# One core of Trainium2: a conditioned decoder block put in source order, with its side work on one paced list

## The chip, the cores and the metric

The kernel runs on one core of a Trainium2 chip. A core has TensorE (matrix products), VectorE (DVE in the profile), ScalarE (ACT), GpSimd (POOL, hardly used here) and SyncE (SP), whose queue issues nearly all transfers. The metric is the device time of one execution in microseconds (us); lower is better.

## The reference, cut to what matters

```python
mod = silu(c) @ w_ada + b_ada                    # c: 4096 numbers, w_ada: 4096 x 12288
shift, scale, gate = split(mod, 3)
h = rmsnorm(x) * norm_g * (1 + scale) + shift    # x: 256 tokens x 4096 channels
a_b, a_c, a_x, a_z, b_v, b_g, b_z = split(h @ w_in)   # 4096 -> 7 x 2048
y_a = a_b * conv3(a_c * a_x) * silu(a_z)         # causal, per channel, width 3
u   = conv31(b_v * sigmoid(b_g)) + bias          # causal, per channel, width 31
y_b = silu(layernorm(u)) * silu(b_z)
x   = x + gate * ([y_a, y_b] @ w_out)            # 4096 -> 4096
return rmsnorm(x) * final_g
```

Everything is float32. Each factor of the large products is split into a high and a low part, and three of the four products of parts are summed, so that one tile of 128 input channels, 128 tokens and 512 output columns costs three TensorE products.

## The kernel before, in words

The input projection has 28 output column tiles `e` of 512 columns and 32 channel tiles `k` of 128 channels. It is not run column by column: `BLOCKS` cuts the 32 channel tiles into six blocks, and in each block all 28 column tiles take in that block's channels, so that the conditioning of a channel tile (`modT`, `gscT`) is needed only when its block begins. `_segments` lists these segments. A segment that goes on with sums of an earlier block starts from the stored sum: `seed` copies `acc[e]` into PSUM on ScalarE, and `take` copies the finished segment back out on ScalarE. Even and odd blocks walk the columns in opposite directions, and the first columns of blocks 0 and 1 stop short by `EARLY`.

A step is one load of weights for two channel tiles (`KD` = 2), 512 KB, and twelve products. `load_w` (lines 131 to 140) issues the load on SP, makes the high part on ScalarE (line 138) and the low part on VectorE (line 139). `products` (142 to 153) issues the twelve products. There are 448 steps for the input projection and 64 for each half of the output projection.

Other work lies beside it. `ada_steps` (179 to 191) computes one column of silu(c) @ w_ada for 128 outputs: four pieces of 1024 rows, each a 512 KB load and one multiply-and-sum pass on VectorE (line 189). 64 such columns are shift and scale (`mod`), 32 are `gate`. `make_h` (233 to 247) turns two channel tiles of x into h. `x_stats` (252 to 272) finds the root mean square by token from the transposed x: squares on ScalarE, sums on VectorE, a product with ones. `glu_B`, `conv_tap`, `norm_B`, `gate_B` and `silu_gate_A` work on finished columns; the width-31 convolution is 120 taps of four ScalarE passes (line 350) and one VectorE add (line 351).

The Python code hands out this work by step: `queue` holds pairs of step and function, and `run_due` calls what is due. The mod pieces are spread so that each channel tile is ready two steps before use, the gate pieces over 170 steps that begin with the last block (`GATE_RUN`), the taps from the first GLU to 43 steps behind the input projection. The tile framework then orders each engine's instructions by its own priorities; that order can differ from the source's. Mod pieces, gate pieces, weights and most x tiles share the seven buffers of `raws`; `big` has 33 slots of 4 KB per partition for h, sums and everything else.

Of the kernel before, what the change touches and what calls it, by code (L numbers as in the profile page):

```python
# [60 lines left out]
def _segments():  # L61
# [23 lines left out]
def decoder_block(ctx: ExitStack, tc: tile.TileContext, x, c, w_mod, w_gate, w_in, w_out, xt, pk, final_g, out):  # L85
    nc = tc.nc
    const = ctx.enter_context(tc.tile_pool(name="const", bufs=1))
    const.tile([P, 420], F32, name="pad")
# [4 lines left out]
    split = ctx.enter_context(tc.tile_pool(name="split", bufs=3))  # L93
# [19 lines left out]
    pks = const.tile([P, PK], F32, name="pks")  # L113
    nc.scalar.dma_start(pks, pk)
# [6 lines left out]
    def rsqrt(y, v, t):  # L121

        nc.scalar.activation(out=t, in_=v, func=AF.Sqrt)
        nc.vector.reciprocal(out=y, in_=t)
        nc.vector.tensor_tensor(out=t, in0=y, in1=y, op=ALU.mult)
        nc.vector.tensor_tensor(out=t, in0=t, in1=v, op=ALU.mult)
        nc.vector.tensor_scalar(out=t, in0=t, scalar1=-0.5, scalar2=1.5, op0=ALU.mult, op1=ALU.add)
        nc.vector.tensor_tensor(out=y, in0=y, in1=t, op=ALU.mult)


    def load_w(src, k0, name, keep=False):
        raw = rawt(f"{name}_r")
        nc.sync.dma_start(raw, src[k0 // KD])
        if keep:
            hi, lo = (bigt(f"{name}_{t}", (P, KD, CT), F32R) for t in "hl")
        else:
            hi, lo = (split.tile([P, KD, CT], F32R, tag=t, name=f"{name}_{t}") for t in "hl")
        nc.scalar.copy(hi, raw)  # L138
        nc.vector.tensor_tensor(out=lo, in0=raw, in1=hi.bitcast(F32), op=ALU.subtract)  # L139
        return hi, lo  # L140

    def products(ps, act, parts, k0, first, last, tokens=range(NS), seeded=False):

        hi, lo = parts
# [19 lines left out]
    pts = [const.tile([P, 4], F32, name=f"part{i}") for i in range(4)]  # L164
    part_no = itertools.count()
    cB = cbc.tile([P, D], F32, name="cB")
    hT = {}

    def broadcast_c():

        for q in range(D // ROW):
            row = bigt(f"crow{q}", (P, ROW))
            nc.sync.dma_start(row[:1], c[:, q * ROW:(q + 1) * ROW])
            ps = pmm.tile([P, NS, CT], F32, tag="ps", name=f"cps{q}")
            for h in range(2):
                nc.tensor.matmul(ps[:, h], ones[:1], row[:1, h * CT:(h + 1) * CT], start=True, stop=True)  # L176
            nc.scalar.activation(out=cB[:, q * ROW:(q + 1) * ROW], in_=ps, func=AF.Silu)

    def ada_steps(name, srcs, bias, dst):

        state = {}

        def step(q):
            raw = rawt(f"{name}_{q}", (P, ROW))
            nc.sync.dma_start(raw, srcs[q])
            if q == 0:
                state["part"] = pts[next(part_no) % 4]
            p = state["part"]
            nc.vector.tensor_tensor_reduce(out=raw, in0=raw, in1=cB[:, q * ROW:(q + 1) * ROW], scale=1.0, scalar=p[:, q - 1:q] if q else bias, op0=ALU.mult, op1=ALU.add, accum_out=dst if q == D // ROW - 1 else p[:, q:q + 1])  # L189

        return [lambda q=q: step(q) for q in range(D // ROW)]

    def mod_steps(k):

        def finish():
# [6 lines left out]
        return work + [finish]  # L202
# [4 lines left out]
    def gate_finish():  # L207
# [69 lines left out]
    for f in first_steps[:-4]:  # L277
        f()
# [344 lines left out]
```

## Time and profile before

| | us |
|---|---|
| median of 3 runs | 1744.9 (1743.64 to 1745.33) |
| profiled execution | 1744.85 |
| its span, first to last instruction | 1743.0 |
| TensorE busy in it | 1644.6 (94%) |
| VectorE busy | 1421.8 (82%) |
| ScalarE busy | 1163.6 (67%) |
| bytes moved | 524.51 MB, 301 GB/s in the mean |

Busy time of TensorE includes the overlap of neighbouring products, so it says less about the pace than the distance between two starts. Shares are means over stages that differ, and the rows below are cut by stage for that reason.

### The profile page before, as it was taken

The numbers are of one execution on the slowest core, as the hardware profiler recorded it, in microseconds if no ns is written. First come the engines' busy times: TensorE is split into PE (matmuls) and PEld (weight loads), VectorE is DVE, ScalarE is ACT, GpSimd is POOL, SyncE is SP. The second block draws the span as 40 slices with busy tenths as digits, with TensorE's granted clock in tenths as the row PEclk, the third lists the DMA queues.
The fourth block names the chain that finished last, engine by engine and source line by source line (L and its number), as shares of the span: only waits on it lengthen the run. The fifth ranks groups of instructions, "written<-read, shape, count | busy, mean of one in ns | idle before, by whom it ended". The sixth has DMA issues, their size and how long they took to land.

```text
span 1743.0 us, 20848 instructions
## 1 busy us (share of the span) xinstructions
PE 1644.6 (94%) x7073; PEld 1323.9 (76%) x7073; DVE 1421.8 (82%) x1707; ACT 1163.6 (67%) x1558; POOL 1.0 (0%) x8
## 2 busy tenths in 40 slices
PE   4799999999999999999999999989998999999997
PEld 1577788888888888888888777766666777778885
DVE  6887777877777777787776899999999999976675
ACT  4555966577666556566556599998898777464453
POOL 0000000000000000000000000000000000000000
PEclk9999999999999999999999999999999999999999
DMA  8998999999999999999998998868887999679663
GB/s 318 319 363 322 325 328 343 321 335 326 327 317 343 330 322 320 324 342 313 333 326 308 332 304 286 300 220 273 271 266 264 314 314 320 221 273 321 201 201 149
DMA packets 146771, 524.51 MB, mean 301 GB/s; under 512 B 16196, under 2 KB 16228, under 8 KB 146664
## 3 DMA queue, kind: packets, MB, share of 16 engines
q1 hardware_dynamic: 146520, 522.81, 86.1%
q8 instruction: 55, 0.90, 0.2%
q10 hardware_dynamic: 144, 0.37, 0.1%
q14 instruction: 52, 0.43, 0.1%
HBM read 518.91 MB, written 4.21 MB: 300 GB/s over the span
## 4 chain that ended last, share of the span: by engine, by line
PE 63%; DVE 18%; issue 10%; ACT 5%; DMA 4%; DVEq 0%; ACTq 0%
PE ps L152 17%; PE ps L153 17%; PE ps L151 17%; DVE w_l L139 5%; DVE cv L351 5%; DVE gate L189 3%; PE pb L151 3%; PE pb L153 3%; PE pb L152 3%; DMA mod<-in_w_mod 2%; ACT w_h L138 2%; ACT pr L350 1%; DVE mod L189 1%; DMA gate<-in_w_gate 1%; PE cps L176 1%
## 5 line engine op out<-in xcount | busy, mean ns | idle before, releaser
L139 DVE TENSOR_TENSOR w_l<-w_r,w_h 128x1024 fp32r<-128x1024 f32 x576 | 702.7, 1226 | 236.1 <-ACT w_h L138 234.3
L138 ACT CAST w_h<-w_r 128x1024 fp32r<-128x1024 f32 x576 | 600.2, 1048 | 260.1 <-PE ps L153 140.7
L152 PE MATMUL ps<-w_l,hT 128*128 128x512 f32 x1792 | 709.4, 396 | 26.5 <-DVE w_l L139 26.3
L151 PE MATMUL ps<-w_h,hT 128*128 128x512 f32 x1792 | 703.4, 393 | 27.6 <-ACT hT L157 18.1
L153 PE MATMUL ps<-w_h,hT 128*128 128x512 f32 x1792 | 703.6, 393 | 1.1 <-DVE hT L158 1.1
L152 PEld LDWEIGHTS ps<-w_l,hT 128*128 128x128 f32 x1792 | 339.2, 189 | 115.4 <-DVE w_l L139 46.2
L151 PEld LDWEIGHTS ps<-w_h,hT 128*128 128x128 f32 x1792 | 339.5, 190 | 104.0 <-ACT hT L157 19.2
L153 PEld LDWEIGHTS ps<-w_h,hT 128*128 128x128 f32 x1792 | 339.6, 190 | 71.9 <-DVE hT L158 3.2
L446 ACT ACTIVATE acc<-ps 128x1024 f32<-128x1024 f32 x163 | 167.4, 1027 | 223.0 <-PE ps L153 222.6
L189 DVE CUSTOM_DVE_ANT_0 mod<-mod,cB,part 128x1024 f32<-128x1024 f32 x192 | 245.7, 1280 | 26.0 <-DMA mod<-in_w_mod 24.1
L350 ACT ACTIVATE pr<-uT,pks 128x255 f32<-128x255 f32 (+14 forms) x480 | 197.0, 488 | 1.8 <-DVE cv L351 1.6
L351 DVE TENSOR_TENSOR cv<-cv,pr 128x1020 f32<-128x1020 f32 (+14 forms) x120 | 140.3, 1169 | 3.6 <-ACT pr L350 3.4
L438 ACT COPY ps<-acc 128x1024 f32<-128x1024 f32 x135 | 137.0, 1016 | 0.4
L189 DVE CUSTOM_DVE_ANT_0 gate<-gate,cB,part 128x1024 f32<-128x1024 f32 x96 | 124.2, 1294 | 1.6 <-DMA gate<-in_w_gate 1.5
L152 PE MATMUL pa<-w_l,yT 128*128 128x512 f32 x256 | 104.0, 406 | 7.9 <-DVE w_l L139 7.4
L151 PE MATMUL pa<-w_h,yT 128*128 128x512 f32 x256 | 100.3, 394 | 1.8 <-ACT w_h L138 1.8
L153 PE MATMUL pa<-w_h,yT 128*128 128x512 f32 x256 | 100.9, 394 | 0.0
L151 PE MATMUL pb<-w_h,yT 128*128 128x512 f32 x256 | 99.7, 389 | 0.0
L152 PE MATMUL pb<-w_l,yT 128*128 128x512 f32 x256 | 99.6, 389 | 0.0
L153 PE MATMUL pb<-w_h,yT 128*128 128x512 f32 x256 | 99.6, 389 | 0.0
L189 DVE CUSTOM_DVE_ANT_0 mod<-mod,cB,pks 128x1024 f32<-128x1024 f32 x64 | 81.9, 1280 | 12.3 <-DMA mod<-in_w_mod 12.3
L152 PEld LDWEIGHTS pa<-w_l,yT 128*128 128x128 f32 x256 | 48.7, 190 | 27.4 <-DVE w_l L139 17.6
(122 smaller groups left out, 678.5 us busy)
## 6 DMA issues: line engine op xcount, KB each, us to landing
w_r<-in_w_in SPq DMA_DIRECT2D x448, 512.0 KB, 5.0
mod<-in_w_mod SPq DMA_DIRECT2D x256, 512.0 KB, 5.1
gate<-in_w_gate SPq DMA_DIRECT2D x128, 512.0 KB, 4.6
w_r<-in_w_out SPq DMA_DIRECT2D x128, 512.0 KB, 4.6
xs<-in_xt SPq DMA_DIRECT2D x8, 512.0 KB, 10.0
xr<-in_x SPq DMA_DIRECT2D x8, 512.0 KB, 6.7
out<-o SPq DMA_DIRECT2D x16, 256.0 KB, 2.9
xc<-in_xt SPq DMA_DIRECT2D x10, 256.0 KB, 4.6
```

What stands on the lines that cost most here:

```text
L138: nc.scalar.copy(hi, raw)
L139: nc.vector.tensor_tensor(out=lo, in0=raw, in1=hi.bitcast(F32), op=ALU.subtract)
L151: nc.tensor.matmul(out, ah, hi[:, i], start=f, stop=False, skip_group_check=seeded)
L152: nc.tensor.matmul(out, ah, lo[:, i], start=False, stop=False, skip_group_check=seeded)
L153: nc.tensor.matmul(out, al, hi[:, i], start=False, stop=l, skip_group_check=seeded)
L176: nc.tensor.matmul(ps[:, h], ones[:1], row[:1, h * CT:(h + 1) * CT], start=True, stop=True)
L189: nc.vector.tensor_tensor_reduce(out=raw, in0=raw, in1=cB[:, q * ROW:(q + 1) * ROW], scale=1.0, scalar=p[:, q - 1:q] if q else bias, op0=A ...
L350: nc.scalar.activation(out=pr[:, j, sh:], in_=u[:, j, :S - sh], func=AF.Copy, scale=cbw[:, 4 * i + j, TAPS - 1 - sh:TAPS - sh])
L351: nc.vector.tensor_tensor(out=o[:, :, sh:], in0=o[:, :, sh:], in1=pr[:, :, sh:], op=ALU.add)
L438: nc.scalar.copy(ps, acc[e])
L446: nc.scalar.activation(out=acc[e], in_=ps, func=AF.Silu if k1 == KT and e >= 24 else AF.Copy)
```

## The change

All engines now run in the order of the source (last lines of the diff), and the source is rewritten so that each piece of side work is a step of its own at a set time. Time is counted in units `now` of one channel tile (six products); 896 units are the input projection, 128 each half of the output projection.

- Blocks are (2, 4, 4, 6, 8, 8); in the first block the first fifteen columns take in channel tile 0 alone (`ALONE`). A step has one or two tiles; a load of one tile is 256 KB.
- Weights are loaded two steps ahead instead of one (`AHEAD`). Weights have four buffers of their own (`raws`), the pieces of w_ada three of 8 KB per partition (`rows`); a piece has 2048 rows, 1 MB. x tiles for h now lie in `big`, which has 34 slots.
- All pieces after channel tile 0, mod first and gate behind it, are one list, `filler`. `run_due` takes the next piece when it is due (on the line `hull`, ahead of all needs) or when two running counts allow it: `vec`, VectorE's planned work, and `load`, the planned transfers at `RATE` MB per us, both against the planned time `FIRST + UNIT * now`.
- h is made in five separate steps of set leads (`H_LEAD`); the taps, the normalisation and the gating of A and B are cut up in the same way, with a producer on one engine and its consumer on the next put some units apart.
- Row statistics of x come from x in its natural layout: squares on ScalarE with a sum by token (`accum_out`), the reciprocal root on 128 x 2 numbers, and two products that spread it over the partitions. They stand between the passes that make `cB`.
- Silu and sigmoid of finished columns are applied while the sum leaves PSUM (`take`), not as passes of their own. Activation tables are asked for ahead of use (`table`).
- In the second half of the output projection the sums start from the first half's (`seed_b`), in place of an add afterwards. The gate vector is stored through ScalarE's queue instead of SP's.

```diff
-BLOCKS = (4, 4, 4, 6, 6, 8)
-
-EARLY = {0: 12, 1: 10}
+BLOCKS = (2, 4, 4, 6, 8, 8)
+
+ALONE = 15
+EARLY = {1: 14}
 KD = 2
-AHEAD = 1
-LEAD = 2
-KEEP = 3
+AHEAD = 2
+ROW = 2048
 HOLD = 5
-ROW = 1024
-GATE_RUN = (0, 170)
-A_SPAN = 5
-
-CONV_END = 43
-NORM_AT = 45
-NORM_SPAN = 20
-LOAD_AT = 1
-TILE_SPAN = 4
+
+
+UNIT = 1.363
+FIRST = 29.0
+RATE = 0.385
+W_LOAD = 0.2622
+ADA_LOAD = 1.0486
+LOW_PART = 0.57
+ADA_SUM = 2.42
+SLACK = 3.0
+
+
+H_LEAD = (9, 6, 4, 2, 1)
+H_DUE = 8
+A_STEP = 3
+CONV_END = 86
+NORM_AT = 88
+NORM_STEP = 2
+LOAD_AT = 2
+TILE_STEP = 3
...
+            if b == 0 and n < ALONE:
+                k1 = 1
...
+def _steps(k0, k1):
+
+    cuts = [k0] + [k for k in range(k0 + 1, k1) if k % KD == 0] + [k1]
+    return [(a, b - a) for a, b in zip(cuts, cuts[1:])]
...
-    big = ctx.enter_context(tc.tile_pool(name="big", bufs=33))
+    big = ctx.enter_context(tc.tile_pool(name="big", bufs=34))
+    raws = ctx.enter_context(tc.tile_pool(name="raws", bufs=4))
+    rows = ctx.enter_context(tc.tile_pool(name="rows", bufs=3))
-    raws = ctx.enter_context(tc.tile_pool(name="raws", bufs=7))
...
+    def run_due():
+
+        nonlocal vec, load
+        t = FIRST + UNIT * now
+        while queue and queue[0][0] <= now:
+            _, cost, f = queue.pop(0)
+            vec = max(vec, t - SLACK) + cost
+            f()
+        while filler:
+            due, mb, cost, f = filler[0]
+            if due > now and (max(vec, t - SLACK) + cost > t + UNIT * KD or max(load, t - SLACK) + mb / RATE > t + UNIT):
+                break
+            filler.pop(0)
+            vec = max(vec, t - SLACK) + cost
+            load = max(load, t - SLACK) + mb / RATE
+            f()
+
+
...
+    def load_w(i):
+        nonlocal vec, load
+        src, k, n = plan[i]
+        raw = raws.tile([P, KD, CT], F32, tag="r", name=f"w{i}_r")
+        part = slice(k % KD, k % KD + n)
+        nc.sync.dma_start(raw[:, part], src[k // KD][:, part])
+        if 0 <= i - len(plan) + KT // 2 // KD < HOLD:
+            hi, lo = (bigt(f"w{i}_{t}", (P, KD, CT), F32R) for t in "hl")
...
+            hi, lo = (split.tile([P, KD, CT], F32R, tag=t, name=f"w{i}_{t}") for t in "hl")
+        nc.scalar.copy(hi[:, part], raw[:, part])
+        nc.vector.tensor_tensor(out=lo[:, part], in0=raw[:, part], in1=hi[:, part].bitcast(F32), op=ALU.subtract)
+        t = FIRST + UNIT * now
+        vec = max(vec, t - SLACK) + LOW_PART * n
+        load = max(load, t - SLACK) + W_LOAD * n / RATE
         return hi, lo
 
...
+        def piece(q):
+            raw = rows.tile([P, ROW], F32, tag="r", name=f"{name}_{q}")
             nc.sync.dma_start(raw, srcs[q])
-            if q == 0:
...
+            nc.vector.tensor_tensor_reduce(out=raw, in0=raw, in1=cB[:, q * ROW:(q + 1) * ROW], scale=1.0, scalar=pt if q else bias, op0=ALU.mult, op1=ALU.add, accum_out=dst if q else pt)
+
+        return [lambda q=q: piece(q) for q in range(D // ROW)]
...
+            nc.scalar.copy(row[:KT], ps[:KT])
+            nc.scalar.dma_start(gate_d.rearrange("(k p) -> k p", p=P), row[:KT])
...
+        def fetch():
+            st["x"] = bigt(f"xc{ks[0]}", (P, n, S))
+            nc.sync.dma_start(st["x"], xt[:, ks[0]:ks[0] + n])
...
+    for q in range(4):
+        ps = pst(f"cps{q}")
+        for h in range(2):
+            nc.tensor.matmul(ps[:, h], ones[:1], crow[q][:1, h * CT:(h + 1) * CT], start=True, stop=True)
+        nc.scalar.activation(out=cB[:, q * 1024:(q + 1) * 1024], in_=ps, func=AF.Silu)
+        for i in ((), (0, 1), (2, 3, 4), (5, 6, 7))[q]:
+            nc.scalar.activation(out=xn[i], in_=xn[i], func=AF.Square, accum_out=sums[:, i % 2, i // 2:i // 2 + 1])
...
+    nc.vector.tensor_reduce(out=v, in_=sums[:, :, :4], axis=mybir.AxisListType.X, op=ALU.add)
+    nc.vector.tensor_scalar(out=v, in0=v, scalar1=1.0 / D, scalar2=EPS, op0=ALU.mult, op1=ALU.add)
+    root()
+    first_mod[0]()
+    rest()
+    yb = bigt("yb", (P, NS, P))
+    for s in range(NS):
+        nc.vector.tensor_scalar(out=yb[:, s], in0=ones, scalar1=y[:, s:s + 1], scalar2=None, op0=ALU.mult)
+    rstd = const.tile([P, S], F32, name="rstd")
+    ps = misc("rstd_ps", (P, S))
+    for s in range(NS):
+        nc.tensor.matmul(ps[:, s * P:(s + 1) * P], yb[:, s], ident, start=True, stop=True)
+    nc.scalar.copy(rstd, ps)
+    table(AF.Silu)
+    first_h[0][0]()
+    first_mod[1]()
+    first_h[1][0]()
+    first_mod[2]()
+    next_w()
+    first_mod[3]()
+    for f, _ in first_h[2:]:
         f()
...
+    vec = load = FIRST - SLACK
+
+
+    work = [f for k in range(1, KT) for f in mod_steps(k)]
+    gates_due = end_in + KT // 2 * NDT - 20
+    need = [(FIRST_USE[k] - H_DUE, len(work) * k // (KT - 1)) for k in range(1, KT)]
+    work += gate_steps()
+    need.append((gates_due, len(work)))
+    hull = [(-3.0, 0)]
+    while hull[-1][1] < len(work):
+        t0, n0 = hull[-1]
+        hull.append(max((p for p in need if p[1] > n0), key=lambda p: ((p[1] - n0) / max(p[0] - t0, 0.1), p[0])))
+    for n, f in enumerate(work):
+        filler.append((float(np.interp(n + 1, [d for _, d in hull], [t for t, _ in hull])), ADA_LOAD, ADA_SUM, f))
+    put(gates_due + 4, gate_store)
+    for ks in [[1]] + [[k, k + 1] for k in range(KD, KT, KD)]:
+        for (f, cost), lead in zip(h_steps(ks), H_LEAD):
+            put(FIRST_USE[ks[0]] - lead, f, cost)
...
+        t = now + 2
+        put(t, gates, 2.3)
+        for j in range(4):
+            t += A_STEP
+            put(t, lambda j=j: turn(j))
+            put(t + 0.1, lambda j=j: tap(j))
+            put(t + 2, lambda j=j: rest(j), 1.15)
...
+        put(now + 2, gated, 1.15)
+        for h in range(2):
+            put(now + 5, lambda h=h: turn(h))
+            put(now + 5.1 + h, lambda h=h: keep(h))
+        put(now + 8, tap)
+        conv_start = conv_start or now + 10
+        w = (conv_end - conv_start) / 4
+        for sh in range(1, TAPS):
+            t = max(now + 10, conv_start + i * w)
+            t += (sh - 1) * (conv_start + (i + 1) * w - t) / (TAPS - 1)
+            put(t, lambda sh=sh, t=t: conv_tap(i, sh, t))
...
+        def add():
+            nc.vector.tensor_tensor(out=o[:, :, sh:], in0=o[:, :, sh:], in1=pr[:, :, sh:], op=ALU.add)
+
+        put(at + 2, add, 1.15)
...
+        yield 4, lambda: mean("mu"), 0.0
+        for i in range(4):
+            yield 5 + i, lambda i=i: center(i), 1.2
+            yield 6.1 + i, lambda i=i: square(i), 0.0
...
+            func = AF.Sigmoid if 20 <= e < 24 else AF.Silu if e >= 24 or 12 <= e < 16 else AF.Copy
...
+            run_due()
+            products(ps, act_h, parts, k, m, k == 0, k + m == k1, seeded=k0 > 0)
+            advance()
...
+    def seed_b(dt):
+        ps = pst(f"pb{dt}")
+        nc.scalar.copy(ps, res[dt])
+        return ps
...
-    with tile.TileContext(nc) as tc:
+    with tile.TileContext(nc, linearize=True) as tc:
```

## Rows read from the trace of the kernel before

**Rows 1.** Windows by stage: busy PE, PEld, DVE, ACT, POOL; clock, DMA share, GB/s.
```profile
0.00:54.00 54.00, 17.99 (x25) 7.89 (x26) 36.73 (x53) 20.97 (x23) 0.99 (x8) 1.00 0.85 316
54.00:972.00 918.00, 912.55 (x3993) 749.52 (x3994) 702.53 (x862) 580.42 (x608) 0.00 (x0) 1.00 0.93 328
972.00:1357.00 385.00, 350.02 (x1481) 273.78 (x1480) 368.71 (x448) 339.74 (x591) 0.00 (x0) 0.96 0.83 280
1357.00:1556.00 199.00, 189.26 (x807) 148.21 (x806) 191.63 (x220) 139.95 (x234) 0.00 (x0) 0.98 0.83 284
1556.00:1731.00 175.00, 174.76 (x775) 144.52 (x772) 117.22 (x112) 79.64 (x100) 0.00 (x0) 1.00 0.68 230
1731.00:1743.00 12.00, 0.00 (x0) 0.00 (x0) 4.96 (x15) 2.87 (x6) 0.00 (x0) 0.66 0.47 180
```

**Rows 2.** Chain that ended last, 1689.9 to 1720: start us, length, what.
```profile
1689.97 0.23 PE pb L151
...
1719.89 0.23 PE pb L151
```

**Rows 3.** Timeline of TensorE, four transposes in a row, first and last.
```profile
1154.57 0.27 PE L315 MATMUL psA<-ident,acc 128*128 128x128 f32 x1
...
1154.89 0.27 PE L316 MATMUL psA<-ident,acc 128*128 128x128 f32 x1
```

**Rows 4.** Waits, 972 to 1357: who waited for whom, us in total, times, longest.
```profile
PE ps L152 <- DVE w_l L139: 21.5, 28, 2.7
```

**Rows 5.** Groups of VectorE and ScalarE, 972 to 1357: busy us, mean ns, idle before.
```profile
L139 DVE TENSOR_TENSOR w_l<-w_r,w_h 128x1024 fp32r<-128x1024 f32 x115 | 140.0, 1226 | 7.4 <-ACT w_h L138 7.4
L351 DVE TENSOR_TENSOR cv<-cv,pr 128x1020 f32<-128x1020 f32 (+14 forms) x84 | 98.0, 1167 | 3.6 <-ACT pr L350 3.4
L189 DVE CUSTOM_DVE_ANT_0 gate<-gate,cB,part 128x1024 f32<-128x1024 f32 x64 | 82.3, 1286 | 1.6 <-DMA gate<-in_w_gate 1.5
L189 DVE CUSTOM_DVE_ANT_0 gate<-gate,cB,pks 128x1024 f32<-128x1024 f32 x21 | 27.0, 1286 | 1.3 <-DMA gate<-in_w_gate 1.3
...
L138 ACT CAST w_h<-w_r 128x1024 fp32r<-128x1024 f32 x115 | 119.2, 1044 | 21.2 <-PE ps L153 16.5 <-DMA w_r<-in_w_in 2.3 <-DVE acc L304 1.7
L446 ACT ACTIVATE acc<-ps 128x1024 f32<-128x1024 f32 x28 | 28.6, 1022 | 13.8 <-PE ps L153 13.4
```

**Rows 6.** Timeline of the start, 0 to 55.
```profile
3.10 13.99 PE L176 MATMUL cps<-crow,ones 1*128 1x512 f32 x16 [3.10 <-DMA crow<-in_c]
...
17.12 1.02 ACT L177 ACTIVATE cB<-cps 128x1024 f32<-128x1024 f32 x1 [1.45 <-PE cps L176]
...
19.93 4.83 ACT L262 ACTIVATE xs<-xs 128x1024 f32<-128x1024 f32 x5
...
39.94 1.75 DVE L124 RECIPROCAL x_rstd<-xq 128x256 f32<-128x256 f32 x1
...
48.73 0.69 DVE L242 TENSOR_TENSOR xs<-xs,x_rstd 128x512 f32<-128x512 f32 x1
...
53.78 0.79 PE L151 MATMUL ps<-w_h,hT 128*128 128x512 f32 x1 [16.74 <-ACT hT L157]
```

**Rows 7.** Transfers by issue, whole span: count, KB each, median us to landing.
```profile
w_r<-in_w_in SPq DMA_DIRECT2D x448, 512.0 KB, 5.0
```

**Rows 8.** Windows by transfer rate; columns as in rows 1.
```profile
5.00:30.00 25.00, 12.08 (x15) 4.25 (x13) 13.15 (x18) 12.94 (x13) 0.00 (x0) 1.00 1.03 418
...
754.00:770.00 16.00, 16.00 (x73) 13.24 (x72) 13.66 (x18) 9.68 (x10) 0.00 (x0) 1.00 1.02 411
...
100.00:950.00 850.00, 847.24 (x3726) 698.48 (x3726) 644.81 (x786) 541.42 (x568) 0.00 (x0) 1.00 0.93 328
```

**Rows 9.** Waits of SP's queue, 100 to 950, longest in total.
```profile
SPq L133 <- DVE w_l L139: 258.9, 174, 3.8
```

**Rows 10.** Timeline of ScalarE in the last block.
```profile
1021.48 1.70 ACT L350 ACTIVATE pr<-uT,pks 128x254 f32<-128x254 f32 x4
1023.07 1.99 ACT L138 CAST w_h<-w_r 128x1024 fp32r<-128x1024 f32 x2
1024.96 1.70 ACT L350 ACTIVATE pr<-uT,pks 128x253 f32<-128x253 f32 x4
```

More of the change, by code (lines that the diff above doesn't have):

```diff
@@ L142, in products, with table, rsqrt_steps, root @@
-    def products(ps, act, parts, k0, first, last, tokens=range(NS), seeded=False):
+    def table(func):
+        nc.scalar.activation(out=dummy, in_=ones[:, 0:1], func=func)
+    def rsqrt_steps(y, v, t):
+        def root():
+            nc.scalar.activation(out=t, in_=v, func=AF.Sqrt)
+        def rest():
+            nc.vector.reciprocal(out=y, in_=t)
+            nc.vector.tensor_tensor(out=t, in0=y, in1=y, op=ALU.mult)
+            nc.vector.tensor_tensor(out=t, in0=t, in1=v, op=ALU.mult)
+            nc.vector.tensor_scalar(out=t, in0=t, scalar1=-0.5, scalar2=1.5, op0=ALU.mult, op1=ALU.add)
+            nc.vector.tensor_tensor(out=y, in0=y, in1=t, op=ALU.mult)
+        return root, rest
@@ new lines, in decoder_block, with put @@
+    plan = [(w_in[e], k, n) for _, e, k0, k1 in SEGS for k, n in _steps(k0, k1)]
+    end_in = sum(n for _, _, n in plan)
+    start_last = sum(k1 - k0 for b, _, k0, k1 in SEGS if b < len(BLOCKS) - 1)
+    conv_end = end_in + CONV_END
+    plan += [(w_out[dt], k0 + k, KD) for k0 in (0, KT // 2) for dt in range(NDT) for k in range(0, KT // 2, KD)]
+    loaded = []
+    step = 0
+    now = 0
+    queue = []
+    filler = []
+    vec = load = 0.0
+    def put(t, f, cost=0.0):
+        queue.append((t, cost, f))
+        queue.sort(key=lambda e: e[0])
@@ new lines, in spread @@
+    def spread(work, start, end, cost=0.0):
+        for i, f in enumerate(work):
+            put(start + i * (end - start) / len(work), f, cost)
+    def run_due():
[13 more added lines that the diff above has]
+            f()
@@ L144, in products, with next_w, advance @@
+    def next_w():
+        while len(loaded) <= min(step + AHEAD, len(plan) - 1):
+            loaded.append(load_w(len(loaded)))
+        return loaded[step]
+    def advance():
+        nonlocal step, now
+        now += plan[step][2]
+        step += 1
+    def products(ps, act, parts, k0, n, first, last, tokens=range(NS), seeded=False):
         hi, lo = parts
-        for i in range(KD):
-            a = act[(k0 + i) // 2]
-            f, l = first and i == 0, last and i == KD - 1
+        for k in range(k0, k0 + n):
+            f, l = first and k == k0, last and k == k0 + n - 1
@@ L274, in decoder_block @@
-    broadcast_c()
-    rstd = x_stats()
-    first_steps = [f for k in range(KD) for f in mod_steps(k)]
-    for f in first_steps[:-4]:
-        f()
-    load_ahead(AHEAD)
-    for f in first_steps[-4:]:
-        f()
-    make_h(0, KD)
-    queue = []
-    def run_due(step):
-        while queue and queue[0][0] <= step:
-            queue.pop(0)[1]()
-    def spread(work, start, end):
-        queue.extend((start + i * (end - start) / len(work), f) for i, f in enumerate(work))
-        queue.sort(key=lambda t: t[0])
@@ L480, in decoder_block @@
     for dt in range(NDT):
[L481 removed]
+        ps = pst(f"pa{dt}")
         for k in range(0, KT // 2, KD):
[L483 to L493 removed]
@@ L494, in decoder_block @@
[L494 to L504 removed]
+            parts = begin_step()
+            run_due()
+            products(ps, yT, parts, k, KD, k == 0, k + KD == KT // 2)
```

460 lines of the change are left out of this document (225 added, 235 removed).

## The prediction

> **What bounds the kernel now.** I read the windows by stage first, because an average over this program hides that its stages have different limits. The stages are cut where the program changes: first product at 54 us, last channel block of the input projection (its last 115 of 448 weight steps) from 972, first half of the output projection from 1357, second half from 1556, tail from 1731 [rows 1].
>
> What a step costs when nothing is in the way comes from the chain inside the second half: between two products that lie 132 apart, 29.92 us pass [rows 2], so 0.2267 us each, 2.720 us for a step of twelve, 1.360 us for one channel tile of the new count ("unit"). The 576 steps give 1567 us, which no part of the change touches. Four transposes in a row start within 0.32 us [rows 3], so 0.107 us each, and the 128 of them 14 us. Held against that, the stages lose (length minus steps times 2.720 minus transposes):
> - before the first product 54 us
> - 54 to 972: 918 − 333 × 2.720 = 12 us
> - 972 to 1357: 385 − 115 × 2.720 − 96 × 0.107 = 62 us
> - 1357 to 1556: 199 − 64 × 2.720 − 32 × 0.107 = 21.5 us
> - 1556 to 1731: 175 − 64 × 2.720 = 1 us, and the tail 12 us
>
> That is 162.5 lost and 1581 worked: 1743.5 against a span of 1743.0. The profiled execution took 1744.85 us, 1.9 more than its span; the median of the runs is 1744.9, so the sum can be compared with the runs as it is.
>
> In the stage 972 to 1357 the loss has a name: VectorE is busy 368.7 of 385 us and ScalarE 339.7 [rows 1], and TensorE waits there for the low parts of the weights [rows 4]. VectorE's work there is 115 low parts (140 us), 84 convolution adds (98) and 85 gate pieces (109) [rows 5]. The gate list was put into exactly the stage that holds the convolution.
>
> **The start.** The c row is spread by sixteen products until 17.1 and the last part of cB stands at 18.1 [rows 6]. The new code puts squares by token between those: with 0.97 us each (five took 4.83 [rows 6]), the last three run behind the last cB, to about 22. From there VectorE is a plain chain in source order: row sum and scaling 0.4, mod piece one, the reciprocal on 2 numbers instead of 256 (it took 1.75 [rows 6]), two small products, pieces 2 to 4, three half-size low parts of 0.6 (a pass over 512, 0.69 in [rows 6], less the 0.1 by which neighbours overlap). A piece of 2048 is in no row: one of 1024 takes 1.29 [rows 5], and an elementwise pass goes from 0.69 at 512 [rows 6] to 1.226 at 1024 elements [rows 5], 1.05 ns each, so I estimate 1.29 + 1.07 = 2.36 us (no less than 2.2, no more than the 2.58 of two old ones). Sum: 22 + 0.4 + 4 × 2.36 + 0.6 + 0.9 + 1.8 = 35.1; by channel 0.6, high part 0.4 and the first product follows at 36.5 instead of 53.8. That gains 17 us. At best 31 (two pieces run before the sums are ready; source order speaks against it), at worst 54 as now.
>
> **Units 0 to 40.** Fifteen segments of a single tile: ScalarE has half a cast (0.55) and an eviction (0.95) in each, 1.5 us against 1.360, so 2 us in all; the twelve segments of two tiles behind unit 40 have a cast, an eviction and a seed, 2.85 against 2.720, 2 us more. VectorE has twelve due pieces until unit 33 (the planner's hull asks for them: 28 us), 35 half low parts (21) and h of four tiles (3): 52 us against 45. A load of half size also shortens SP's lead: it may be four weight loads ahead, which is 5.4 us here and 10.9 later, while a 512 KB load of now lands after 5.0 [rows 7]. I take 10 us for all of it: 7 for VectorE, 3 for transfers, and nothing for ScalarE, which catches up in the same waits. Bounds 3 and 20.
>
> **Units 40 to 690: the paced list.** I worked through the planner's own budget: after unit 160 no piece is due and it admits ten per 40 units, always because of its transfer budget, so 0.2622 + 1.0486 / 4 MB a unit, with the x tiles 0.526 MB per 1.360 us = 386 GB/s, for some 655 units counted from unit 35. Now the mean is 328 at a share of 0.93 [rows 8]. Can the queue give 386? Before the products it gave 418 over 25 us, and beside a TensorE that was busy throughout 411 over 16 us [rows 8]; SP meanwhile waits mostly for VectorE to give buffers back, not for transfers [rows 9]. So the 328 is what was asked for. I take 5 us for stretches where it falls short; bounds 0, and 85 if 328 / 0.93 = 353 were the ceiling (655 × (0.526 / 0.353 − 1.360)).
>
> The Trainium skill, page "DMA: Bandwidth & Descriptors", section "Bandwidth", says that about 358 GB/s on the HBM side is what binds a load into SBUF. By that figure this stretch would cost 72 us instead of 5. The trace does not agree over 16 and 25 us (411 and 418); no row shows it for longer.
>
> **Where a new block of h begins (units 448 and 672)** the 34 slots hold 28 sums, four old h tiles, and now the x tiles too, which had slots of their own. An x load waits until TensorE frees an old h tile, and SP queues the weight loads behind it. SP then has two steps of lead, 5.4 us, for landing 5, cast 1.05 and low part 1.22 [rows 5]: 4 us each time, 8 in all; bounds 0 and 16.
>
> **The last block (units 672 to 896).** By the planner's list some 168 of 188 pieces are done when it begins, so VectorE loses most of the 109 us: it keeps 112 low parts at 1.14 (128), 84 adds at 1.15 (96), group A and GLU 38 (four times 8.2 and 1.2: two products, eight taps of 0.4, four products of 0.36, two low parts of 0.6), h 5 and 20 pieces (45) = 312 us against 316 of TensorE. ScalarE is next: from the first tap at unit 698 to unit 896 TensorE needs 198 × 1.360 + 10 = 279 us, and ScalarE 99 casts at 0.95 (94; two take 1.89 in [rows 10]), 50 evictions and seeds at 0.93 (46; 1.02 in [rows 5], less the overlap), 84 taps at 1.59 [rows 10] (133), GLU 12 (8 copies, 16 first taps of 0.5), A 11 (16 taps of 0.4, 8 high parts) = 296. Separate Silu and Sigmoid passes are gone (8 × 1.05), the taps are not. Source order leaves no way to push a tap behind a cast, so the 17 us are lost; with VectorE as full as TensorE, I add 9 for waits across engines. 26 us, from 10 to the 62 of now.
>
> **First half of the output projection.** VectorE: low parts 73, taps 41, normalisation and gates 38 (30 passes of 0.6 to 1.2) = 152 of 178 us, without the gate pieces that fill it to 191.6 of 199 now [rows 1]. But the norm steps lie in 48 units (65 us) with 27 low + 35 other, every product of theirs at a fixed place in TensorE's order. 6 us instead of 21.5; bounds 1 and 21.5.
>
> **Second half and tail.** Seeding replaces one add of 1.2 per tile on VectorE by a copy on ScalarE; TensorE loses 1 us now and hides both (a seed that is late would cost its 1 us, eight times at most). Tail unchanged, 12. The gate vector's store goes to ScalarE's queue, behind casts and in front of none that a product waits for within two steps; its readers come 18 units (24 us) later, so it costs nothing; without that cover it would be the length of one small store.
>
> **Sum.** 1581 + 36.5 + 10 + 5 + 8 + 26 + 6 + 1 + 12 + 1.9 = 1687.4. In order: work, start, units 0 to 40, queue, new blocks of h, last block, norm, second half, tail, what lies outside the span.
>
> **Rivals.**
> - **All of it hidden.** Taps fit because TensorE is slower than its pace anyway, no turn stalls: block 10, others at their lower bounds (3, 0, 0, 1): 1581 + 36.5 + 3 + 10 + 1 + 1 + 12 + 1.9 = 1646 to about 1662. For it: the next stage leaves ScalarE idle for 59 us [rows 1]; against it: in source order a tap can't move there.
> - **Source order blocks.** Four queues wait for each other in the last block and the norm; the losses of now remain (62 and 21.5): 1687 + 36 + 15 = 1738. For it: both engines at 97 to 106% there; against it: 109 us less on VectorE.
> - **The start is not earlier**: the pieces of the first tile arrive or run late, first product near 54: 1705. For it: this chain is all VectorE.
> - **The queue cannot hold 386 GB/s** (the other side). TensorE then runs at the queue's pace for 655 units. At 353 it costs 85 instead of 5: 1767, slower than before. It decides from 62 us of loss, 0.526 / (1.360 + 62 / 655), that is below 361 GB/s. For it: 353 from share and rate [rows 8]; against: 411 beside TensorE.
>
> By the Trainium skill's 358 (named above) that case would end at 1754.
>
> **Numbers.** My sum's surroundings (1664 to 1712) 0.50, all hidden 0.15, start late 0.10 (it lies inside these surroundings), blocked 0.15, queue too slow 0.10. The range leaves out the slow queue and the best end of the hidden case: 1650 to 1738. 0.2% is about what a measurement of this kernel can tell from no change (3.5 us). Slower: the slow queue and a little of the blocked case, 0.11; within: 0.03; faster 0.86.
>
> **What would show it.** First product at 36 (30 to 42 right); x products per 50 us near 220 and 380 to 390 GB/s from 100 to 950 if the queue holds; there, waits of TensorE on low parts and a rate flat at 350 to 365 with a DMA share of 1 if it does not. In the last block waits of TensorE for high parts (ScalarE), no longer for low ones alone; gate pieces almost absent. Wrong if the loss sits before unit 690, or if VectorE is still the one at 99% in the last block.

## The result, and the profile after

| | us |
|---|---|
| before, median of 4 runs | 1744.9 (1743.64 to 1745.33) |
| after, median of 4 runs | 9082.2 (9077.7 to 9088.95) |
| ratio after to before | 5.206, 95% interval 5.197 to 5.215 |
| predicted | 1687 (1650 to 1738) |

The forecast is off by more than a factor of five, and no rival named comes near. None of the signs that the prediction looked for is there: the first product starts at 131.1 us (36 was looked for), the 50 us shown below hold 36 products (near 220), and the transfers come to 58 GB/s in the mean (380 to 390). The page of the changed kernel, its busy times and its chain:

```profile
PE 2967.6 (33%) x7069; PEld 2110.9 (23%) x7069; DVE 1445.1 (16%) x1329; ACT 1278.2 (14%) x1587; POOL 1.1 (0%) x8
...
DMA 35%; PE 33%; DVE 16%; ACT 14%; issue 2%; ACTq 0%; DVEq 0%; SPq 0%; POOL 0%; POOLq 0%
...
w_r<-in_w_in SPq DMA_DIRECT2D x433, 512.0 KB, 3.6
mod<-in_w_mod SPq DMA_DIRECT2D x128, 1024.0 KB, 4.9
gate<-in_w_gate SPq DMA_DIRECT2D x64, 1024.0 KB, 4.9
w_r<-in_w_out SPq DMA_DIRECT2D x128, 512.0 KB, 3.6
w_r<-in_w_in SPq DMA_DIRECT2D x30, 256.0 KB, 2.5
```

Put the two lists beside each other. The engines' shares of the chain equal their shares of busy time: 33, 16 and 14%. The loads listed take 433 × 3.6 + 192 × 4.9 + 128 × 3.6 + 30 × 2.5 = 3035 us, and with PE, DVE and ACT the sum is 8726 of 9082. When the busy times of all engines and the landings of all loads add up to the span, nothing runs beside anything else. The timeline of one step shows it:

```profile
3004.65 0.63 PE L243 MATMUL ps<-w_l,hT 128*128 128x512 f32 x1
3005.08 0.62 PE L244 MATMUL ps<-w_h,hT 128*128 128x512 f32 x1
3005.73 0.33 SPq L210 DMA_DIRECT2D w_r<-in_w_in  x1
3009.37 1.04 ACT L215 CAST w_h<-w_r 128x1024 fp32r<-128x1024 f32 x1 [9.21 <-DMA w_r<-in_w_in]
3010.45 1.23 DVE L216 TENSOR_TENSOR w_l<-w_r,w_h 128x1024 fp32r<-128x1024 f32 x1 [11.34 <-ACT w_h L215]
3011.70 0.33 SPq L268 DMA_DIRECT2D mod<-in_w_mod  x1
3016.47 2.35 DVE L269 CUSTOM_DVE_ANT_0 mod<-mod,cB,pks 128x2048 f32<-128x2048 f32 x1 [4.80 <-DMA mod<-in_w_mod]
3018.75 0.08 DVE L269 DVE_READ_ACCUMULATOR2_ANT pts<- 128x1 f32 x1
3018.89 0.29 PEld L242 LDWEIGHTS ps<-w_h,hT 128*128 128x128 f32 x1 [13.90 <-DVE pts L269]
3018.89 0.79 PE L242 MATMUL ps<-w_h,hT 128*128 128x512 f32 x1 [13.19 <-DVE pts L269]
```

A load is issued only when the last product has ended; its cast follows the landing, the low part the cast, the next load the low part, and so on to the next products, 13 us later. None of these products needs the load of 3005.73, which is for two steps later, nor the piece of `mod`. Two rows of waits say the same, the second of SP's queue:

```profile
PE ps L242 <- DVE pts L269: 1362.5, 93, 47.1
```

```profile
SPq L210 <- PE ps L244: 5624.0, 463, 18.8
```

TensorE waits 93 times for `pts`, which no product reads, and SP waits for products, where it waited for VectorE to hand back buffers [rows 9]. Windows: 50 us in the middle, and the whole span.

```profile
3000.00:3050.00 50.00, 15.72 (x36) 11.10 (x36) 7.92 (x6) 5.34 (x6) 0.00 (x0) 0.60 0.23 73
...
0.00:9082.00 9082.00, 2967.63 (x7069) 2110.85 (x7069) 1445.06 (x1329) 1278.22 (x1587) 1.11 (x8) 0.62 0.18 58
```

The granted clock is 0.62 in the mean, against 1.00 in most stretches of before [rows 1]. On both sides of the pause of 13 us shown above (3000.3 to 3005.5 and 3019 to 3022) it is 0.50, the lower of its two levels (1.2 of 2.4 GHz), and the products start 0.43 us apart in place of 0.2267 [rows 2].

### The profile page after: what moved, and what is told of

Read it like the earlier page. It is cut to its first block, busy times and chain, and to the rows that moved or that the text cites. A ratio compares the mean times of both kernels' runs of the same rounds, so it can differ in the third digit from the quotient of the medians.

```text
span 9082.3 us, 20232 instructions
## 1 busy us (share of the span) xinstructions
PE 2967.6 (33%) x7069; PEld 2110.9 (23%) x7069; DVE 1445.1 (16%) x1329; ACT 1278.2 (14%) x1587; POOL 1.1 (0%) x8
## 4 chain that ended last, share of the span: by engine, by line
DMA 35%; PE 33%; DVE 16%; ACT 14%; issue 2%; ACTq 0%; DVEq 0%; SPq 0%; POOL 0%; POOLq 0%
DMA w_r<-in_w_in 18%; PE ps L242 10%; DVE w_l L216 8%; PE ps L243 8%; PE ps L244 8%; DMA mod<-in_w_mod 7%; ACT w_h L215 7%; DMA w_r<-in_w_out 5%; DMA gate<-in_w_gate 3%; DVE mod L269 3%; ACT pr L494 3%; ACT acc L603 2%; DVE gate L269 2%; DVE cv L497 2%; ACT ps L593 2%
## 5 line engine op out<-in xcount | busy, mean ns | idle before, releaser
L242 PE MATMUL ps<-w_h,hT 128*128 128x512 f32 x1792 | 1153.9, 644 | 4721.6 <-DVE pts L269 1362.5
L242 PEld LDWEIGHTS ps<-w_h,hT 128*128 128x128 f32 x1792 | 556.7, 311 | 5092.8 <-issue 2090.0
L216 DVE TENSOR_TENSOR w_l<-w_r,w_h 128x1024 fp32r<-128x1024 f32 (+1 forms) x591 | 708.3, 1199 | 6165.8 <-ACT w_h L215 6165.8
L215 ACT CAST w_h<-w_r 128x1024 fp32r<-128x1024 f32 (+1 forms) x591 | 604.3, 1022 | 6943.2 <-DMA w_r<-in_w_in 5604.5
L243 PE MATMUL ps<-w_l,hT 128*128 128x512 f32 x1792 | 1058.8, 591 | 0.0
L244 PE MATMUL ps<-w_h,hT 128*128 128x512 f32 x1792 | 1031.1, 575 | 0.0
L243 PEld LDWEIGHTS ps<-w_l,hT 128*128 128x128 f32 x1792 | 570.1, 318 | 120.2
L244 PEld LDWEIGHTS ps<-w_h,hT 128*128 128x128 f32 x1792 | 554.6, 309 | 160.7
L242 PE MATMUL pa<-w_h,yT 128*128 128x512 f32 x256 | 161.0, 629 | 545.6 <-ACT pr L494 316.3
L242 PE MATMUL pb<-w_h,yT 128*128 128x512 f32 x256 | 162.7, 636 | 494.6 <-DVE w_l L216 139.6
L269 DVE CUSTOM_DVE_ANT_0 mod<-mod,cB,pts 128x2048 f32<-128x2048 f32 x64 | 150.5, 2352 | 382.9 <-DMA mod<-in_w_mod 382.9
L269 DVE CUSTOM_DVE_ANT_0 mod<-mod,cB,pks 128x2048 f32<-128x2048 f32 x64 | 150.5, 2351 | 367.9 <-DMA mod<-in_w_mod 367.9
L244 PE MATMUL pb<-w_h,yT 128*128 128x512 f32 x256 | 146.4, 572 | 0.0
L244 PE MATMUL pa<-w_h,yT 128*128 128x512 f32 x256 | 142.1, 555 | 0.0
```

Of the source, the lines that this page charges most:

```text
L215: nc.scalar.copy(hi[:, part], raw[:, part])
L216: nc.vector.tensor_tensor(out=lo[:, part], in0=raw[:, part], in1=hi[:, part].bitcast(F32), op=ALU.subtract)
L242: nc.tensor.matmul(out, ah, hi[:, i], start=f, stop=False, skip_group_check=seeded)
L243: nc.tensor.matmul(out, ah, lo[:, i], start=False, stop=False, skip_group_check=seeded)
L244: nc.tensor.matmul(out, al, hi[:, i], start=False, stop=l, skip_group_check=seeded)
```

## The experiments

All ran beside the kernel before; ratios are to its runs on the same chip.

**Is it the one chain?** Theory A: `linearize=True` ties every instruction to the one before it in the source, on whatever engine, transfers included. Rival: the new order itself, or the new pieces, are that slow. e1 and e2 take the flag away, e3 and e4 give the old kernel the flag, or the source's order alone.

```diff
 e1, e4 (after, before)
+    with tile.TileContext(nc) as tc:
+        with tc.manual_schedule():   # source order on each engine; waits for data and buffers alone
+            decoder_block(tc, **args)
 e2 (after)
-    with tile.TileContext(nc, linearize=True) as tc:
+    with tile.TileContext(nc) as tc:
 e3 (before)
-    with tile.TileContext(nc) as tc:
+    with tile.TileContext(nc, linearize=True) as tc:
```

> The changed kernel with the same order on each engine, but each instruction waits only for its data, its buffers and its own engine; the flag's waits on the instruction before it in the source, on another engine, are gone. Theory A (the flag makes one chain of all instructions over all engines, and that is the whole loss): 1640 to 1740 us, the sum of the prediction, first product near 36, units 40 to 690 at 380 to 390 GB/s. Rival B (the order on each engine blocks the queues, whoever waits): stays above 5000. Rival C (the paced list asks for more transfers than the queue gives): 1750 to 1800, flat at 350 to 365 GB/s.

Measured: 1811.0 us (1.037, interval 1.035 to 1.040).

> The changed kernel without the flag: the framework chooses each engine's order again. Theory A: 1640 to 1760, within 60 us of the run with source order. Rival B: near 1700 here while the run with source order stays high. Rival C: 1750 or more in both.

Measured: 1816.1 (1.042, 1.040 to 1.044).

> The kernel before with the flag alone. Theory A: a sum of everything, one thing at a time: 576 steps of load 3.6, high 1.05, low 1.23 and twelve products 5.1 (half clock), 384 pieces of 3.6 and 1.35, 120 taps of 2.9, 300 copies of 1: 6300 + 1900 + 350 + 300 and small ones, 9000 to 10000 us. Rivals B and C: below 2500, since the kernel before has neither the paced list nor steps cut up for it.

Measured: 9547.7 (5.475, 5.462 to 5.487). Its page looks like that of the changed kernel:

```profile
PE 2972.1 (31%) x7073; PEld 2120.1 (22%) x7073; DVE 1504.9 (16%) x1707; ACT 1273.1 (13%) x1557; POOL 1.1 (0%) x8
...
DMA 37%; PE 31%; DVE 15%; ACT 13%; issue 2%; ACTq 0%; SPq 0%; DVEq 0%; POOL 0%; POOLq 0%
```

> The kernel before in source order on each engine, without the flag's chain. Theory A: some per cent beside 1745, either way; its source puts whole chains (a GLU, a tile of A, make_h) in one place, so engines wait for each other there: I expect 1800 to 2000. Rival B: above 3000.

Measured: 1858.9 (1.066, 1.064 to 1.067).

The flag alone makes the old kernel 5.5 times slower, source order without it 7%, and without the flag the changed kernel is some 4% above before: the chain is shown to be the loss. But e1 and e2 missed theory A's numbers, and in number rival C (the queue gives too little) is nearer. Freed of the chain the change is still 67 us slower than before and 124 over the forecast. The rest of the study is about these 124, in e1; what holds e2 back was not followed. Windows of e1 by the predicted stages (start; units 0 to 40; 40 to 690; 690 to 896; the two halves of the output projection), and 50 us in which TensorE is full:

```profile
0.00:36.30 36.30, 15.25 (x21) 6.12 (x21) 13.06 (x23) 19.75 (x33) 0.99 (x8) 1.00 0.87 329
36.30:99.90 63.60, 60.63 (x241) 46.52 (x241) 53.65 (x57) 45.17 (x54) 0.00 (x0) 1.00 0.94 369
99.90:1088.50 988.60, 943.99 (x3902) 750.61 (x3901) 770.00 (x709) 567.91 (x601) 0.00 (x0) 0.97 0.93 346
1088.50:1409.70 321.20, 306.78 (x1334) 243.95 (x1332) 278.02 (x280) 300.33 (x535) 0.00 (x0) 0.99 0.64 210
1409.70:1606.00 196.30, 187.25 (x799) 150.04 (x797) 151.35 (x138) 149.64 (x251) 0.00 (x0) 0.98 0.65 203
1606.00:1802.70 196.70, 189.13 (x782) 151.64 (x780) 112.72 (x111) 85.54 (x109) 0.00 (x0) 0.95 0.60 195
600.00:650.00 50.00, 50.00 (x215) 40.24 (x215) 41.45 (x39) 29.93 (x30) 0.00 (x0) 1.00 0.99 371
```

The last 50 us in the kernel before:

```profile
600.00:650.00 50.00, 50.00 (x222) 41.44 (x221) 38.35 (x47) 29.47 (x30) 0.00 (x0) 1.00 0.95 328
```

Two things stand out. In e1's last row TensorE is busy all 50 us at full clock and yet does 215 products; before, 222. And units 40 to 690 took 988.6 where 884 is the work. Rival C is not the reason: with TensorE busy throughout the loads run at 371 GB/s, above C's 350 to 365, and they fall where TensorE stops (261 from 700 to 750).

**The distance of products.** The products of e1 start further apart than before: 234.1 ns against 227.2 (mean over all starts 200 to 260 ns apart). The first and the thirteenth of a row, before and then in e1:

```profile
599.73 0.39 PE L151 MATMUL ps<-w_h,hT 128*128 128x512 f32 x1
...
602.45 0.39 PE L151 MATMUL ps<-w_h,hT 128*128 128x512 f32 x1
```

```profile
599.83 0.40 PE L242 MATMUL ps<-w_h,hT 128*128 128x512 f32 x1
...
602.64 0.39 PE L242 MATMUL ps<-w_h,hT 128*128 128x512 f32 x1
```

The load of the queue does not matter: e1 does 215 in 50 us beside 371 GB/s and also, from 1650 to 1700, beside 229. What differs is where the tiles lie in a partition of the on-chip memory: the pools stand in another order. In e1 the weights' parts (`split`) lie at multiples of 4096 bytes and the tiles of h 3424 above one.

```diff
 e5 (e1)
+    const.tile([P, 8], F32, name="shift")            # 32 bytes: h to 3456 above
 e6 (before)
-    const.tile([P, 420], F32, name="pad")
+    const.tile([P, 428], F32, name="pad")            # 32 bytes: both operands
```

> The changed order without the chain ran in 1811.0, and its products follow each other at 0.234 us with TensorE full, where the kernel before has 0.226. Between the two the tiles of h (the stationary operand) moved from addresses that are multiples of 4096 bytes to addresses 3424 above such a multiple, which is 32 above a multiple of 64; the weights' two parts stayed at multiples of 4096. Here one unused tile of 32 bytes is added to the pool of constants, so that h lies 3456 above, a multiple of 128; nothing else changes. Theory P (the address of h within a small unit sets the pitch): pitch back to 0.226 to 0.227, 6912 products gain 45 to 52 us, 1759 to 1768. Theory Q (only the multiple of 4096 counts): pitch stays 0.234, 1811 +- 4. Theory R (the pitch comes from something else that runs beside it, the queue or the order): pitch stays 0.234, 1811 +- 4. Q and R are told apart by the next kernel.

Measured: 1804.5 (1.034, 1.032 to 1.036), 232.4 ns, 217 products in the same 50 us.

> The kernel before with its unused tile of 1680 bytes made 1712, so that every tile behind it, both operands of the products among them, lies 32 bytes above a multiple of 4096. Its order and its queues stay. Theories P and Q: the pitch goes from 0.226 to 0.234 or more (both operands are moved here), and where TensorE sets the time, about 5000 of the 6912 products, that costs 40 us or more: 1780 to 1800; with a second price for the weights' parts up to 1840. Theory R: no change, 1744 +- 3.

Measured: 1743.9 (1.000, 0.999 to 1.002), 227.2 ns, 223 products. P and Q fall: no address is bad in itself. R would have e5 unchanged, and it did move. What gave the next theory was e1's own trace: those of its last products whose weights' parts lie in the pool of h, and so share its remainder, follow at 227 ns, between others at 231 to 234. So theory U, the two operands' remainders of 4096 must be the same, against V, the place of the weights' parts.

```diff
 e9 (e1): split directly behind const, both operands at 3424
 e10 (e1): split behind rows, with a gap of 672 bytes
 e11 (before): the same gap ahead of split
+    gap = ctx.enter_context(tc.tile_pool(name="gap", bufs=1))
+    gap.tile([P, 168], F32, name="shift")
     split = ctx.enter_context(tc.tile_pool(name="split", bufs=3))
```

> The changed order without the chain (1811.0; pitch of its products 0.234 us), with the pool of the weights' parts moved behind the constants and nothing else: both operands of a product now lie 3424 bytes above a multiple of 4096, and the weights' parts stay below the tiles of h, at 7520 to 32096. What is known: the address alone does not set the pitch (32 bytes on all of the kernel before changed nothing), and in the changed kernel the last products, whose weights' parts lie in the pool of h, already follow at 0.227. Theory U (the pitch rises when the two operands have different remainders of 4096): pitch 0.227, 1811 less 45 to 50, 1760 to 1768. Theory V (the place of the weights' parts, low in the memory, sets it): pitch 0.234, 1811 +- 5.

> The changed order without the chain, with the pool of the weights' parts moved to the end of the memory, behind all others, as it is in the kernel before, and a gap of 672 bytes before it, so that the difference of the remainders stays 672 as it was. Theory U: pitch stays 0.234, 1811 +- 5. Theory V: pitch 0.227, 1760 to 1768.

> The kernel before with the same gap of 672 bytes before its pool of the weights' parts, which stays at the end: the parts lie 672 above a multiple of 4096, h at the multiple. Its order stays. Theory U: the pitch goes from 0.227 to 0.234 where TensorE is full, about 5000 of the products, 35 us or more: 1775 to 1790. Theory V: no change, 1744 +- 3.

Measured: e9 1776.4 (1.019, 1.017 to 1.020), e10 1816.2 (1.042, 1.040 to 1.043), e11 1774.6 (1.019, 1.017 to 1.021). The same 50 us of e9, e10 and e11:

```profile
600.00:650.00 50.00, 50.00 (x222) 41.42 (x221) 43.24 (x42) 30.27 (x32) 0.00 (x0) 1.00 1.00 386
```

```profile
600.00:650.00 50.00, 50.00 (x215) 40.22 (x214) 41.44 (x39) 29.90 (x30) 0.00 (x0) 1.00 1.00 374
```

```profile
600.00:650.00 50.00, 50.00 (x215) 40.20 (x214) 35.73 (x43) 29.46 (x30) 0.00 (x0) 1.00 0.91 313
```

| kernel | weights' parts | h | ns per product |
|---|---|---|---|
| before | 0, at the end | 0 | 227.2 |
| e6 | 32, at the end | 32 | 227.2 |
| e9 | 3424, ahead of h | 3424 | 227.0 |
| e12 (below) | 3424, at the end | 3424 | 227.0 |
| e5 | 0, ahead of h | 3456 | 232.4 |
| e1 | 0, ahead of h | 3424 | 234.1 |
| e10 | 4032, at the end | 3360 | 234.1 |
| e11 | 672, at the end | 0 | 234.1 |

By the distance of products U holds in both kernels and at both places, V at neither. In time it is worth 35 us in e1 and 31 in e11; e10 and e11 lie within 1 us of U's ranges, and U's 45 to 50 for e9 was too much (TensorE does not set the time everywhere). One thing U leaves open: 4096 is the size of a tile. Inside a tile the operands of single products start at multiples of 512 bytes (`products` cuts them so), at equal remainders of the tiles all these differences give 227, and so a remainder of 512 fits the runs as well.

**The stops.** The timeline of e1 at the turn to the block of unit 448:

```profile
718.21 0.80 PE L244 MATMUL ps<-w_h,hT 128*128 128x512 f32 x1 [4.59 <-DVE hT L251]
718.80 0.63 PE L242 MATMUL ps<-w_h,hT 128*128 128x512 f32 x1
...
722.88 1.04 ACT L215 CAST w_h<-w_r 128x1024 fp32r<-128x1024 f32 x1 [5.07 <-PE ps L244]
...
723.96 1.23 DVE L216 TENSOR_TENSOR w_l<-w_r,w_h 128x1024 fp32r<-128x1024 f32 x1 [5.20 <-ACT w_h L215]
...
725.10 0.68 DVE L251 TENSOR_TENSOR hT<-xc,hT 128x512 fp32r<-128x512 f32 x1
...
725.84 0.50 PE L244 MATMUL ps<-w_h,hT 128*128 128x512 f32 x1 [2.14 <-DVE hT L251]
```

Read it backwards. The product at 725.84 waits for the low part of h; VectorE made that behind the low part of weights; that waited for their cast; and the cast at 722.88 waited for TensorE to free a buffer. Those weights are for two steps later. In source order they stand ahead of the h that the next products need, so TensorE waits for itself. Behind the stop before this one it starts again at the lower clock (granted 0.50 from 718.3 to 722, 0.43 us a product). e7 swaps the two in the source; e8 adds the 32 bytes of e5.

```diff
-            parts = begin_step()        # load, cast and low part of weights two steps ahead
-            ...
             run_due()                   # parts of h, pieces, norm, gates
+            parts = begin_step()
```

> The changed order without the chain (1811.0) in which each step's due work (parts of h, pieces of conditioning, the norm and the gate of the second half) now stands ahead of the next weights' load, cast and low part, not behind them; the addresses stay as they were, so the pitch of 0.234 stays. Theory S (at the turns of the blocks and at the norm TensorE waits for the low part of h or of y, because that stands behind a cast of weights that itself waits for TensorE to free its buffer): the stops at the turns (about 230 products short by the windows of 50 us, 54 us) and at the norm (about 105 short, 24 us) mostly go, 1735 to 1770. Rival T (the stops come from h itself being too late, its loads, conditioning rows or buffers): little moves, 1795 to 1815.

> The changed order without the chain with both edits: 32 bytes more in the pool of constants, and each step's due work ahead of the next weights. If P and S both hold the gains add, 45 to 52 for the pitch and 40 to 75 for the stops: 1685 to 1725, faster than the kernel before and near what was predicted for the change (1687). If only one holds, 1735 to 1770; if neither, 1811.

Measured: e7 1752.5 (1.004, 1.003 to 1.006), 58 us less than e1: S holds, and T, by which little moves, falls. e8 1745.2 (1.000, 0.999 to 1.001), as forecast for one of the two holding: P had fallen. e12 joins e7 with one remainder, as in e9, but with `split` at the end:

> The changed order without the chain, each step's due work ahead of the next weights (1752.5 alone), and the pool of the weights' parts moved to the end without a gap, so that both operands have the remainder 3424: by either theory the pitch is 0.227. 6912 products at 7 ns less, where TensorE is full: 1700 to 1712, 2 per cent faster than the kernel before. If the queue or the engines that make the operands then end last (the queue was full at 380 GB/s from 300 to 1000), part of it goes into waits: 1712 to 1735.

Measured: 1712.0 (0.983, 0.981 to 0.984): the two mends add up (99 us, 58 and 35 singly), and the changed order is now 1.7% under the kernel before. Its largest hole is one window:

```profile
1500.00:1550.00 50.00, 37.54 (x140) 30.08 (x141) 21.02 (x26) 18.26 (x24) 0.00 (x0) 0.80 0.39 124
```

This is the end of the norm. By the source's own due times the low part of the first pair of y is made at unit 128 of the output projection (due at 127.5, and steps begin at even units), and the products at 128 read it.

```diff
 e13, e15 (e12)
-CONV_END = 86
-NORM_AT = 88
+CONV_END = 80
+NORM_AT = 82
 e14, e15 (e12)
-H_LEAD = (9, 6, 4, 2, 1)
-H_DUE = 8
+H_LEAD = (11, 8, 6, 4, 3)
+H_DUE = 10
```

> The kernel of 1712.0 (changed order without the chain, due work ahead of the next weights, one remainder for both operands) with the end of the convolution and the start of the norm 6 units earlier (80 and 82 in place of 86 and 88); nothing else. Theory W (the stop of 19 us at the norm comes from due times: the first pairs of the second half's operand fall due in the very step that uses them): most of it goes, 1694 to 1703. Rival X (the taps then crowd VectorE and ScalarE, which is busy 48 to 49 of 50 us there, and TensorE loses in the convolution what it gains at the norm): 1708 to 1720.

> The kernel of 1712.0 with each part of h two units earlier (leads 11, 8, 6, 4, 3 in place of 9, 6, 4, 2, 1, and the conditioning due 10 units ahead in place of 8). Theory Y (the stops at the turns, about 25 us, come from due times): 1698 to 1706. Rival Z (the parts of h wait for free buffers of the pool of 34, which nearly all hold partial sums, and the conditioning due earlier asks more of a full queue): 1710 to 1720.

> Both edits on the kernel of 1712.0. If W and Y hold: 1680 to 1696, near the predicted 1687. If one holds: 1694 to 1706. If neither: 1708 to 1725.

Measured: e13 1697.9 (0.974, 0.972 to 0.975), W holds; this is the fastest version, 2.6% under the kernel before. e14 1711.0 (0.981, 0.979 to 0.983), no gain, Y falls. e15 1700.4 (0.975, 0.974 to 0.976), no better than e13. In e14 the wait at the turn moved and did not go: SP's wait for a free buffer for x is longer, with the weights queued behind it, while TensorE's wait for h there (3.8 us in e12) is gone and waits for the weights' parts (2.5 us) stand in its place. SP's queue, 640 to 720, e12 and then e14:

```profile
SPq L316 <- PE ps L244: 8.1, 1, 8.1
```

```profile
SPq L316 <- PE ps L244: 10.0, 1, 10.0
```

That is what rival Z said of buffers. Its other half, the conditioning due earlier, was not tried by itself, and neither was one more buffer.

## Why the prediction was wrong

**The step that failed** is the reading of the flag, `linearize=True` in the last line of the diff. The prediction took "All engines now run in the order of the source" as one order per engine ("Source order leaves no way to push a tap behind a cast"), with four queues that still overlap. It is one order for all of them, transfers included. The rival "Source order blocks" had the right suspicion and the wrong size: 51 us in two stages, where it is all of the overlap, 7271 us against e1. Nothing in the trace of before could show it; a price for a wait after each of some 10,000 instructions could have been bounded from rows (landing of a load 5.0 [rows 7], a cast and a low part of 1.04 and 1.23 [rows 5], 576 times, alone make some 4,200), and no such rival was priced.

**The sum behind it** can be held against e13, which has the change's order and pieces without the chain, and the three mends (remainder, order within a step, norm six units earlier). Its windows, cut at the starts of products 1, 241, 4141, 5377, 6145 and the last:

```profile
0.00:36.40 36.40, 15.24 (x21) 6.11 (x21) 13.04 (x23) 19.74 (x33) 0.99 (x8) 1.00 0.90 336
36.40:100.10 63.70, 59.39 (x240) 46.47 (x241) 55.13 (x59) 45.70 (x56) 0.00 (x0) 1.00 0.96 367
100.10:1009.40 909.30, 893.49 (x3902) 732.49 (x3901) 773.25 (x713) 567.36 (x599) 0.00 (x0) 1.00 0.98 379
1009.40:1322.80 313.40, 297.69 (x1334) 240.14 (x1333) 279.71 (x282) 303.45 (x547) 0.00 (x0) 1.00 0.66 214
1322.80:1507.90 185.10, 180.62 (x811) 148.74 (x809) 149.45 (x141) 147.40 (x245) 0.00 (x0) 1.00 0.66 203
1507.90:1682.00 174.10, 174.10 (x768) 144.09 (x768) 107.36 (x102) 83.54 (x105) 0.00 (x0) 1.00 0.68 221
600.00:650.00 50.00, 50.00 (x223) 41.41 (x222) 43.07 (x40) 30.52 (x31) 0.00 (x0) 1.00 1.00 384
```

Each loss is a length less its units × 1.360 and its transposes × 0.107, as in the prediction:

| term | predicted | e1 | e13 |
|---|---|---|---|
| start | 36.5 | 36.3 | 36.4 |
| units 0 to 40 | 10 | 9 | 9 |
| units 40 to 690: queue 5, new blocks 8 | 13 | 105 | 25 |
| last block | 26 | 31 | 23 |
| first half of output projection | 6 | 19 | 8 |
| second half | 1 | 23 | 0 |
| tail | 12 | 13 | 13 |

- Right in place and size: the start (piece of 2048 rows: 2.35 us, estimated 2.36; the terms written down add up to 36.1, not 36.5), units 0 to 40 as a sum (its split into 7 and 3 was not tested), and the last block with ScalarE as the fullest engine (303 of 313 us) and VectorE behind it. What TensorE waits for there (1009 to 1323) is ScalarE, as predicted, but its copies of the seeds and not its casts of weights:

```profile
PE ps L242 <- ACT ps L593: 13.5, 13, 1.8
```

- Right: the queue. e13 moved 379 GB/s over 909 us, and 384 in 50 us of full TensorE, so the rival that needed less than 361 falls. The Trainium skill's page "DMA: Bandwidth & Descriptors", section "Bandwidth", gives about 358 GB/s on the HBM side as what binds. These measured rates do not agree with it.
- Too small: the turns of the blocks. The prediction looked for two stops of 4 us, behind an x load. It did not follow the order within a step, and so missed that the low part of h stands behind a cast that waits for TensorE; of e1's 105 the distance of products is 29 (3900 × 7.4 ns), and the swap of e7 takes out 53. 25 us remain in e13. The two predicted stops are 12 of them: at units 448 and 672 the starts that come more than 260 ns apart lose 5.8 and 5.9 us, with one gap of 4.0 and 4.1 us among them, and the x load does wait as predicted (8.1 us in e12 and e13). Their windows in e13, and TensorE's main wait in units 40 to 690, which is for h itself and not for weights:

```profile
650.00:700.00 50.00, 46.15 (x196) 37.43 (x195) 42.92 (x43) 30.62 (x37) 0.00 (x0) 0.97 0.92 362
950.00:1000.00 50.00, 46.08 (x196) 37.40 (x195) 42.63 (x41) 28.63 (x35) 0.00 (x0) 0.97 0.93 363
```

```profile
PE ps L244 <- DVE hT L251: 13.7, 7, 3.9
```

  The rest lies mostly at units 41 to 85, 140 and 280, at which the sum put nothing. The second half's 23 were, apart from 6 for the distance of products, a matter of due times (17 in e12, 0 in e13).
- Missed: the place of the pools in memory, which the whole diff changes. It has no term in the sum, and it costs 35 us in e1.

Start, queue and last block were argued for a kernel that overlaps, so their being right in e13 does not make the forecast for the change right. What remains in units 40 to 690 beyond the predicted 13 is placed but not explained; e14 shows only that earlier due times do not remove the stops.

## What to carry to other kernels

Look first at whether the busy times of all engines and the landings of transfers add up to the span: then nothing overlaps, and an option that orders the program has to be understood before any term of a sum is made. In a program of strict order, follow for each wait what stands ahead of the needed instruction on every engine: work for later that waits for TensorE, ahead of work that TensorE needs next, makes it wait for itself (58 us here, by two lines that change places). When pools are moved, compare the distance of products before and after, not the busy share, which is 100% in both.

## What the hardware showed that was not expected

- TensorE's distance between products of 128x128 by 128x512 depends on how the addresses of its two operands lie to each other: 227 ns if the tiles of both have the same remainder of 4096 bytes, 232 to 234 if that of the moving operand (the weights' parts) is 640 or 672 above that of the stationary one (h). Multiples of 512 between the operands are harmless, as inside the tiles. Why, the runs do not show, nor which other differences are harmless.
- One core's loads held 384 GB/s beside a full TensorE, and 386 in e9, at a share of 1.00; the kernel before moved 328 in the mean [rows 8].
